# The norms of a two-layer diffusion block: high halves straight from PSUM, one weight wait more, and a regrouped product

## The chip, the cores and the metric

The kernel runs on one core of one Trainium2 chip. The metric is the device time of one execution, in microseconds (us). Before the change it is 1271.71 us, the median of three runs (1271.14 to 1274.31).

## The reference

Two layers of a hybrid block act on 256 latent tokens and 256 context tokens, each of width 1024. In each layer, an input modulated by `sc1` and `sh1` goes through one input projection to attention heads and gated DeltaNet heads, and through one output projection back; the sum is normalised. Then a squared-ReLU MLP follows, with a modulation and a norm of its own:

```python
x_lat = layer_norm(DEEPNORM_ALPHA * x_lat + g1 * y_lat, ln1_g[l], ln1_b[l])
x_lat = layer_norm(DEEPNORM_ALPHA * x_lat
                   + g2 * squared_relu_mlp(x_lat * (1.0 + sc2) + sh2, w_mlp1[l], w_mlp2[l]),
                   ln2_g[l], ln2_b[l])
```

The context goes through the same in layer 0 with modulations of its own. Layer 1 gives only the latent tokens. All is float32.

## The kernel before

**Products.** A float32 product is made of three matmuls in a rounded float32 type (fp32r): each operand is split into a high half (the value rounded) and a low half (the rest), and `mm3` (L274 on) issues high x high, one mixed term, and the other (L276, L277, L278). So every weight tile of 128x1024 goes through `wload` (L244 on): a DMA into `wraw` (4 buffers), a copy on ScalarE that rounds it to `whi` (L250), and a subtraction on VectorE that gives `wlo` (L252). There are 3 buffers of whi and wlo, and 6 more that can be filled ahead of a stage (NHOLD). 224 weights go this way.

**Tiles.** The 512 tokens are four tiles `t` of 128; t = 0 and 1 are context, t = 2 and 3 latent. Token-major products write PSUM tiles `pst` (128x512, two halves of the width per tile), and `z_update` (L1054 on) adds them to the residual x on VectorE in two instructions (`ztmp` at L1058, x at L1060 or L1062), here called z rows.

**The norm.** `ln` (L390 on) takes the statistics of x on VectorE (L394, L396, L399), `rs` on GpSimd (POOL), `nm` on VectorE (L411). Then the first half of x is normalised on ScalarE (L414) and the second on VectorE (L415). TensorE transposes x in eight 128x128 pieces into two PSUM tiles `lnp`, one for each half, each a bank (L422). Out of these comes the next product's operand, modulated per column by A and B: a float32 copy `lnh`, of which the first half is written by ScalarE in four pieces (L427) and the second by VectorE in four pieces (L429). From lnh, ScalarE makes the high half `hhi`, 128x512 at a time (L433), and VectorE the low half `hlo` (L434). Ten norms do this: layer 0's first norm for four tiles, its second norm for four, layer 1's first norm for t = 2 and 3. Afterwards `affine` (L439, L440) applies the norm's own gain and bias to x with VectorE, off the way to the product.

**The order.** A list scheduler puts the instructions of each engine into one static queue. An edge, `tc.issue_after`, can hold an instruction behind another in the queue without any data between them: `fence` (L251, L412, L1057) holds the instructions of VectorE that are traced after a norm behind that norm's nm. A bit mask in CFG says which: 1 is wlo, 2 is ztmp. `f12` is the mask of layer 1's first norm, t = 2; `f13` that of t = 3, `f02` that of layer 0's, t = 3 (keys (1, 1, 2) and so on in L412).

**The product after layer 1's first norm.** For t = 2 and 3 the first four weights of the MLP are used token-major (`mlp1_tok`, L1244 on): h is the stationary operand of 24 matmuls of 128x512 into one PSUM tile `pm1`, with two pieces k of h per weight and `mm3` for each k. The remaining weights follow in 128x256 products.

**MLP rows.** In the MLP, ScalarE and VectorE turn `pm` into `ah` and `al` (mr at L1239 and al at L1242 on VectorE).

Of the kernel before, what the change touches and what calls it, by code (L numbers as in the profile page):

```python
# [15 lines left out]
AF = mybir.ActivationFunctionType  # L16
ALU = mybir.AluOpType
# [5 lines left out]
KT = 8  # L23
# [17 lines left out]
    "ord0": "HHBHHCXfNffffNNfffffNKQffaaaKaQfaaKfaQfaffaaKfaQfaZaaaZZfffafffZ",  # L41
    "ord1": "BHHHHCNfffXNfffNfNfKfQfaafKfQfaaKfQKfaQfaafffZZZaZ", "tr": 7, "tr2": 2, "acc": 2, "g": 3, "n": 3,
    "late": 3, "tord": (0, 1, 2, 3), "adab": "n", "depth": 3, "npre": 8, "pre1": (0, 2, 3), "vt": "n",
    "tm": 1, "tmh": (2, 3), "gt": 2, "f02": 1, "f12": 2, "f13": 1,
    "start": "WLmmmWme01WLmmmm2eLmbm0mmbLe1m2m0mme12012bb", "cin": 7, "rows": 1,
}
C_ID, C_U, C_L, C_CM, C_COS, C_SIN, C_END = 0, 128, 256, 384, 448, 704, 960
# [129 lines left out]
def body(ctx, tc, a, out, dump=None):  # L177
    nc = tc.nc
    V, S, G, PE, SP = nc.vector, nc.scalar, nc.gpsimd, nc.tensor, nc.sync
# [47 lines left out]
    def small(shape, name, dt=F32, bufs=3):  # L227
        return P0.tile(shape, dt, name=name, tag="sm_" + name, bufs=bufs)
# [44 lines left out]
    last_mm = []  # L273

    def mm3(o, l, r, start, stop):
        PE.matmul(o, l[0], r[0], start=start, stop=False)  # L276
        PE.matmul(o, l[0], r[1], start=False, stop=False)  # L277
        last_mm[:] = [PE.matmul(o, l[1], r[0], start=False, stop=stop).ins]  # L278

    def new_h(pool, n=NTOK):  # L280
        return (pool.tile([128, KT, n], F32R, name="hhi", tag="hhi"),
                pool.tile([128, KT, n], F32R, name="hlo", tag="hlo"))
# [104 lines left out]
    def seg(t):  # L387
        return 1 if t < 2 else 0

    def ln(MP, l, which, t, z, cols, h, c_=0, fin=None):  # L390
# [6 lines left out]
        rs = small([128, 1], "rs")  # L397
# [15 lines left out]
        n = z  # L413
        S.activation(n[:, :512], z[:, :512], AF.Identity, bias=nm, scale=rs)  # L414
        V.tensor_scalar(n[:, 512:], z[:, 512:], rs, nm, op0=ALU.mult, op1=ALU.add)  # L415
        if h is not None:
            A, B = cols
            s = seg(t)
            for i in range(2):
                p = sn("lnp").rearrange("p (j c) -> p j c", j=4)  # L420
                for j in range(4):
                    PE.transpose(p[:, j], n[:, 512 * i + 128 * j:512 * i + 128 * j + 128], ident)  # L422
                hf = MP.tile([128, 4, 128], F32, name="lnh", tag="lnh", bufs=2)
                for j in range(4):
                    k = 4 * i + j
                    if i == 0:
                        S.activation(hf[:, j], p[:, j], AF.Identity, bias=B[:, s, k:k + 1], scale=A[:, s, k:k + 1])  # L427
                    else:
                        V.tensor_scalar(hf[:, j], p[:, j], A[:, s, k:k + 1], B[:, s, k:k + 1], op0=ALU.mult, op1=ALU.add)  # L429
                c0 = 128 * t - c_  # L430
                dh = h[0][:, 4 * i:4 * i + 4, c0:c0 + 128]
                dl = h[1][:, 4 * i:4 * i + 4, c0:c0 + 128]
                S.activation(dh, hf, AF.Copy)  # L433
                V.tensor_tensor(dl, hf, dh.bitcast(F32), op=ALU.subtract)  # L434

    def affine(x, rows):
# [671 lines left out]
    with tc.tile_pool(name="xin", bufs=1, reuse_waits="tile") as XP, \  # L1108
# [30 lines left out]
        with tc.manual_schedule(engines={nc.tensor.engine}):  # L1139
            for c in CFG["start"]:  # L1140
                i = cnt.get(c, 0)
# [29 lines left out]
    for l in range(L):  # L1171
# [9 lines left out]
        with tc.tile_pool(name="mlp%d" % l, bufs=1, reuse_waits="tile") as MP:  # L1181
# [27 lines left out]
            A, B, sh = mod_cols(l, 2)  # L1209
            fuse_cols(A, B, sh, l, 0)  # L1210
            h2 = new_h(MP, width)
# [32 lines left out]
            def mlp1_tok(ws, t):  # L1244
                c0 = 128 * t - t0
                ps = sm("pm1")
                for i in range(4):
                    for k2 in range(2):
                        k, c = 2 * i + k2, slice(512 * k2, 512 * k2 + 512)
                        mm3(ps, (h2[0][:, k, c0:c0 + 128], h2[1][:, k, c0:c0 + 128]), (ws[i][0][:, c], ws[i][1][:, c]), k == 0, k == KT - 1)  # L1250
                r = MP.tile([128, 512], F32, name="mrt", tag="ztmp", bufs=2)
                S.activation(r, ps, AF.Relu)
                V.tensor_tensor(r, r, r, op=ALU.mult)
                return t, r, last_mm[0]
# [108 lines left out]
```

## Time and profile before

| | |
|---|---|
| median of 3 runs | 1271.71 us (1271.14 to 1274.31) |
| the profiled execution | 1274.56 us, its span 1272.8 us |
| TensorE / VectorE / ScalarE / GpSimd busy | 96% / 68% / 49% / 7% |
| mean granted clock of TensorE | 0.981 |
| chain of work that ended last | TensorE 75%, VectorE 10%, ScalarE 5% |
| largest group on VectorE | wlo, L252, 224 times, 275.5 us |
| largest group on ScalarE | whi, L250, 224 times, 237.0 us |

The profile is of one execution. Its span is what lies between its first and its last instruction, and the execution takes 1.8 us more than that. TensorE's clock has two levels, 2.4 GHz and 1.2 GHz, and the column PEclk gives what was granted as a share of the full one. In a timeline, a row's start and duration stand first; "x4" merges four instructions that follow each other, and the bracket at the end names an idle time before the row and what ended it. Rows of one engine can overlap a little, as an instruction's end lies after the start of the next.

### The profile page before, as it was taken

Reading aid. Unit: us, or ns where it says so; the run is one execution under the profiler, and the core shown is the slowest. Engines: PE = TensorE matmul, PEld = TensorE weight load, DVE = VectorE, ACT = ScalarE, POOL = GpSimd, SP = SyncE. Lnnn points to the kernel's source line nnn. Section 1 sums busy time; section 2 is a strip of 40 time slices with the busy share of each in tenths; the row PEclk is TensorE's granted clock in tenths of the full one; section 3 lists DMA queues with packets and bytes.
Section 4 is the critical chain, followed back from the end, with each engine's and each line's share of the span. In section 5 each row is a group of like instructions: output and inputs, shape, how many; then the busy total and the mean of one; then the engine's idle time right before and its main releaser. Section 6 shows DMA issues by size and latency. Waiting matters only on the chain.

```text
span 1272.8 us, 20344 instructions
## 1 busy us (share of the span) xinstructions
PE 1217.7 (96%) x7848; PEld 988.5 (78%) x7848; DVE 862.5 (68%) x1716; ACT 619.0 (49%) x1131; POOL 90.2 (7%) x98
## 2 busy tenths in 40 slices
PE   7999899999999999999999999899899998999997
PEld 3676568887878987787788889675578886898996
DVE  4798497766479954444444588994876768766677
ACT  2465737665446632322322456567455654544552
POOL 0133000100101000000000001221000110000000
PEclk9999998999999999999999999999889998999999
DMA  9624470215166633534533355236621357455562
GB/s 329 225 67 129 148 251 19 63 50 183 63 230 190 222 120 118 160 127 130 158 128 100 100 182 199 70 113 203 219 89 36 112 177 280 166 185 195 183 187 95
DMA packets 62721, 190.92 MB, mean 150 GB/s; under 512 B 7808, under 2 KB 17824, under 8 KB 62624
## 3 DMA queue, kind: packets, MB, share of 16 engines
q1 hardware_dynamic: 62624, 189.62, 45.4%
q8 instruction: 62, 1.02, 0.3%
q14 instruction: 35, 0.29, 0.1%
HBM read 187.46 MB, written 2.13 MB: 149 GB/s over the span
## 4 chain that ended last, share of the span: by engine, by line
PE 75%; DVE 10%; ACT 5%; POOL 2%; issue 2%; DMA 2%; SPq 0%; DVEq 0%; POOLq 0%; ACTq 0%
PE pst L276 8%; PE pst L277 8%; PE pst L278 8%; PE pm L276 7%; PE pm L278 7%; PE pm L277 7%; PE pss L717 3%; PE adaps L303 3%; DVE wlo L252 2%; PE pss L697 1%; DVE XT L533 1%; PE psn L276 1%; PE pss L714 1%; PE psn L278 1%; ACT MY L822 1%
## 5 line engine op out<-in xcount | busy, mean ns | idle before, releaser
L252 DVE TENSOR_TENSOR wlo<-wraw,whi 128x1024 fp32r<-128x1024 f32 x224 | 275.5, 1232 | 187.6 <-ACT whi L250 187.0
L250 ACT ACTIVATE whi<-wraw 128x1024 fp32r<-128x1024 f32 x224 | 237.0, 1060 | 316.8 <-PE pst L278 172.0
L276 PE MATMUL pm<-hhi,whi 128*128 128x256 f32 (+1 forms) x544 | 176.4, 324 | 0.8 <-ACT whi L250 0.7
L278 PE MATMUL pm<-hhi,wlo 128*128 128x256 f32 (+1 forms) x544 | 174.5, 321 | 0.0
L277 PE MATMUL pm<-hlo,whi 128*128 128x256 f32 (+1 forms) x544 | 174.4, 321 | 0.0
L276 PE MATMUL pst<-whi,ah 128*128 128x512 f32 x384 | 150.0, 391 | 0.0
L277 PE MATMUL pst<-wlo,ah 128*128 128x512 f32 x384 | 149.5, 389 | 0.0
L278 PE MATMUL pst<-whi,al 128*128 128x512 f32 x384 | 149.1, 389 | 0.0
L276 PEld LDWEIGHTS pm<-hhi,whi 128*128 128x128 f32 x544 | 103.5, 190 | 14.4 <-issue 5.8
L278 PEld LDWEIGHTS pm<-hhi,wlo 128*128 128x128 f32 x544 | 103.6, 190 | 7.8
L277 PEld LDWEIGHTS pm<-hlo,whi 128*128 128x128 f32 x544 | 103.6, 190 | 7.2
L276 PEld LDWEIGHTS pst<-whi,ah 128*128 128x128 f32 x384 | 72.1, 188 | 15.5 <-issue 0.8
L278 PEld LDWEIGHTS pst<-whi,al 128*128 128x128 f32 x384 | 72.1, 188 | 15.1
L277 PEld LDWEIGHTS pst<-wlo,ah 128*128 128x128 f32 x384 | 72.1, 188 | 14.5
L276 PE MATMUL psg<-hhi,whi 128*128 128x512 f32 (+1 forms) x216 | 78.1, 363 | 4.7 <-ACT XT L531 2.3
L277 PE MATMUL psg<-hlo,whi 128*128 128x512 f32 (+1 forms) x216 | 78.1, 362 | 0.2 <-DVE hlo L1119 0.2
L278 PE MATMUL psg<-hhi,wlo 128*128 128x512 f32 (+1 forms) x216 | 77.9, 361 | 0.4 <-DVE wlo L252 0.4
L533 DVE SCALAR_TENSOR_TENSOR XT<-U,cw,XT 128x512 f32<-128x512 f32 (+1 forms) x96 | 67.4, 723 | 1.9 <-ACT XT L531 1.6
L1241 ACT ACTIVATE ah<-mr 128x256 fp32r<-128x256 f32 (+1 forms) x68 | 33.4, 492 | 65.6 <-DVE mr L1239 65.6
L303 PE MATMUL adaps<-wraw,scT 128*32 128x256 f32 x640 | 56.4, 395 | 3.4 <-DMA wraw<-w_ada 3.2
L231 POOL TENSOR_TENSOR rs<-ve,mh 128x1 f32<-128x1 f32 x12 | 12.5, 1043 | 630.9 <-DVE bmv L396 362.2
L1242 DVE TENSOR_TENSOR al<-mr,ah 128x256 fp32r<-128x256 f32 (+1 forms) x68 | 35.1, 517 | 24.3 <-ACT ah L1241 24.2
(671 smaller groups left out, 2418.8 us busy)
## 6 DMA issues: line engine op xcount, KB each, us to landing
wraw<-w SPq DMA_DIRECT2D x140, 512.0 KB
wraw<-w_ada SPq DMA_DIRECT2D x80, 512.0 KB
wraw<-w_gdn SPq DMA_DIRECT2D x27, 512.0 KB
wraw<-w_out SPq DMA_DIRECT2D x24, 512.0 KB
xa<-w_ada SPq DMA_DIRECT2D x32, 256.0 KB
wraw<-w_vz SPq DMA_DIRECT2D x16, 512.0 KB
wraw<-w_na SPq DMA_DIRECT2D x16, 512.0 KB
lnrow<-lnr SPq DMA_DIRECT2D x8, 512.0 KB
```

Of the source, the lines that this page charges most:

```text
L250: S.activation(hi, r, AF.Copy)
L252: V.tensor_tensor(lo, r, hi.bitcast(F32), op=ALU.subtract)
L276: PE.matmul(o, l[0], r[0], start=start, stop=False)
L277: PE.matmul(o, l[0], r[1], start=False, stop=False)
L278: last_mm[:] = [PE.matmul(o, l[1], r[0], start=False, stop=stop).ins]
L303: PE.matmul(st["ps"][32 * g:32 * g + 32, :256], scT[:, k, :], w[:, 256 * g:256 * g + 256], start=(k == 0), stop=(k == 7), tile_position=(0 ...
L533: V.scalar_tensor_tensor(av, cin[:, sg:, kk:kk + 256], cw[:, b, kk:kk + 1], av, op0=ALU.mult, op1=ALU.add)
L697: PE.matmul(ps[:, :128 * nkt], nqT[hp][:, a2, qs], nkT[hp][i][:, a2, :128 * nkt], start=i == 0, stop=i == 1)
L714: PE.transpose(ps[:, 128 * kt_:128 * kt_ + 128], p_[:, 128 * kt_:128 * kt_ + 128], ident)
L717: PE.matmul(ps[:, 0:65], p_[:, 128 * kt_:128 * kt_ + 128], nv[:, kt_, hd], start=kt_ == 0, stop=kt_ == nkt - 1)
L1241: S.activation(ah, r, AF.Copy)
L1242: V.tensor_tensor(al, r, ah.bitcast(F32), op=ALU.subtract)
```

## The change

Three things are changed. In `ln`, both halves are now treated alike: for each of the eight pieces ScalarE writes hhi straight out of PSUM (L438 of the changed kernel), VectorE writes lnh out of the same PSUM piece (L439), and hlo is subtracted as before (L440). CFG sets f12 to 3, so that the three wlo that are traced after t = 2's norm in layer 1 come behind its nm as well as the ztmp. And `mlp1_tok` issues, for two weights at a time (four column pieces), first the products with hhi and then the four with hlo.

```diff
-    "tm": 1, "tmh": (2, 3), "gt": 2, "f02": 1, "f12": 2, "f13": 1,
+    "tm": 1, "tmh": (2, 3), "gt": 2, "f02": 1, "f12": 3, "f13": 1,
...
+    def mm3_of(o, ls, rs, start, stop):
+
+        n = len(ls)
+        for i in range(n):
+            PE.matmul(o, ls[i][0], rs[i][0], start=start and i == 0, stop=False)
+            PE.matmul(o, ls[i][0], rs[i][1], start=False, stop=False)
+        for i in range(n):
+            last_mm[:] = [PE.matmul(o, ls[i][1], rs[i][0], start=False, stop=stop and i == n - 1).ins]
...
                 hf = MP.tile([128, 4, 128], F32, name="lnh", tag="lnh", bufs=2)
-                for j in range(4):
-                    k = 4 * i + j
-                    if i == 0:
-                        S.activation(hf[:, j], p[:, j], AF.Identity, bias=B[:, s, k:k + 1], scale=A[:, s, k:k + 1])
-                    else:
-                        V.tensor_scalar(hf[:, j], p[:, j], A[:, s, k:k + 1], B[:, s, k:k + 1], op0=ALU.mult, op1=ALU.add)
                 c0 = 128 * t - c_
                 dh = h[0][:, 4 * i:4 * i + 4, c0:c0 + 128]
                 dl = h[1][:, 4 * i:4 * i + 4, c0:c0 + 128]
-                S.activation(dh, hf, AF.Copy)
+                for j in range(4):
+                    k = 4 * i + j
+                    S.activation(dh[:, j], p[:, j], AF.Identity, bias=B[:, s, k:k + 1], scale=A[:, s, k:k + 1])
+                    V.tensor_scalar(hf[:, j], p[:, j], A[:, s, k:k + 1], B[:, s, k:k + 1], op0=ALU.mult, op1=ALU.add)
                 V.tensor_tensor(dl, hf, dh.bitcast(F32), op=ALU.subtract)
...
-                for i in range(4):
-                    for k2 in range(2):
-                        k, c = 2 * i + k2, slice(512 * k2, 512 * k2 + 512)
-                        mm3(ps, (h2[0][:, k, c0:c0 + 128], h2[1][:, k, c0:c0 + 128]), (ws[i][0][:, c], ws[i][1][:, c]), k == 0, k == KT - 1)
+                for i in range(0, 4, 2):
+                    ls = [(h2[0][:, k, c0:c0 + 128], h2[1][:, k, c0:c0 + 128]) for k in range(2 * i, 2 * i + 4)]
+                    rs = [(ws[j][0][:, c:c + 512], ws[j][1][:, c:c + 512]) for j in (i, i + 1) for c in (0, 512)]
+                    mm3_of(ps, ls, rs, i == 0, i == 2)
```

Three places in the queues show what it does to the order. The number at the end of a name tells instances apart, and the words in brackets name the engines or DMA queues whose semaphores the instruction waits for.

VectorE in layer 0's second norm, t = 0 and 1, up to the weight that TensorE needs next (wlo_6886 in the kernel before). Before:

```order
L434 TENSOR_TENSOR hlo_6566<-lnh_6745,hhi_6565 128x4x128 [waits Activation_49]
L252 TENSOR_TENSOR wlo_6860<-wraw_6857,whi_6859 128x1024 [waits DMAHW3_49,Activation_49]
L434 TENSOR_TENSOR hlo_6566<-lnh_6757,hhi_6565 128x4x128 [waits Activation_49]
L1058 TENSOR_TENSOR ztmp_6875<-pst2_6801,grow_4711 128x512 [waits PE_49]
L429 TENSOR_SCALAR lnh_6794<-lnp_6789,mA_6559,mB_6560 128x128 [waits DVE_49]
L429 TENSOR_SCALAR lnh_6794<-lnp_6789,mA_6559,mB_6560 128x128 x2
L434 TENSOR_TENSOR hlo_6566<-lnh_6782,hhi_6565 128x4x128 [waits Activation_49]
L429 TENSOR_SCALAR lnh_6794<-lnp_6789,mA_6559,mB_6560 128x128
L1062 TENSOR_TENSOR x2_3615<-x2_3615,ztmp_6875 128x512 [waits DVE_49]
L1058 TENSOR_TENSOR ztmp_6878<-pst2_6802,grow_4711 128x512 [waits PE_49]
L252 TENSOR_TENSOR wlo_6886<-wraw_6883,whi_6885 128x1024 [waits DMAHW4_49]
```

After, where the same weight is wlo_6922:

```order
L1064 TENSOR_TENSOR ztmp_6911<-pst2_6837,grow_4735 128x512
L439 TENSOR_SCALAR lnh_6812<-lnp_6807,mA_6583,mB_6584 128x128 [waits Activation_49]
L439 TENSOR_SCALAR lnh_6827<-lnp_6822,mA_6583,mB_6584 128x128 [waits Activation_49]
L1068 TENSOR_TENSOR x2_3615<-x2_3615,ztmp_6911 128x512 [waits DVE_49]
L439 TENSOR_SCALAR lnh_6812<-lnp_6807,mA_6583,mB_6584 128x128 [waits Activation_49]
L439 TENSOR_SCALAR lnh_6827<-lnp_6822,mA_6583,mB_6584 128x128 [waits Activation_49]
L440 TENSOR_TENSOR hlo_6590<-lnh_6812,hhi_6589 128x4x128 [waits DVE_49]
L439 TENSOR_SCALAR lnh_6827<-lnp_6822,mA_6583,mB_6584 128x128 [waits Activation_49]
L1064 TENSOR_TENSOR ztmp_6914<-pst2_6838,grow_4735 128x512
L440 TENSOR_TENSOR hlo_6590<-lnh_6827,hhi_6589 128x4x128 [waits DVE_49]
L1068 TENSOR_TENSOR x3_3617<-x3_3617,ztmp_6914 128x512 [waits DVE_49]
L252 TENSOR_TENSOR wlo_6922<-wraw_6919,whi_6921 128x1024 [waits DMAHW4_49]
```

Both halves of the norm stand in VectorE's queue now, piece by piece and each behind a wait for ScalarE; the weight comes behind the last hlo and the last x row, where before it stood ahead of them.

ScalarE in layer 1's first norm, t = 2. Before:

```order
L414 ACTIVATE x2_10085<-x2_10085,nm_10177,rs_10173 128x512 [waits DVE_49]
L427 ACTIVATE lnh_10186<-lnp_10181,mB_10038,mA_10037 128x128 [waits PE_49]
L427 ACTIVATE lnh_10186<-lnp_10181,mB_10038,mA_10037 128x128 x3
L433 ACTIVATE hhi_10043<-lnh_10186 128x4x128 [waits Activation_49]
L433 ACTIVATE hhi_10043<-lnh_10198 128x4x128 [waits DVE_49]
```

After:

```order
L423 ACTIVATE x2_10133<-x2_10133,nm_10225,rs_10221 128x512 [waits DVE_49]
L438 ACTIVATE hhi_10091<-lnp_10229,mB_10086,mA_10085 128x128 [waits PE_49]
L438 ACTIVATE hhi_10091<-lnp_10244,mB_10086,mA_10085 128x128 [waits PE_49]
L438 ACTIVATE hhi_10091<-lnp_10229,mB_10086,mA_10085 128x128 [waits DVE_49]
L438 ACTIVATE hhi_10091<-lnp_10244,mB_10086,mA_10085 128x128 [waits DVE_49]
L250 ACTIVATE whi_10370<-wraw_10368 128x1024 [waits DMAHW1_49]
L438 ACTIVATE hhi_10091<-lnp_10229,mB_10086,mA_10085 128x128 [waits DVE_49]
L438 ACTIVATE hhi_10091<-lnp_10244,mB_10086,mA_10085 128x128 [waits DVE_49]
```

The pieces of the two PSUM tiles (lnp_10229 and lnp_10244) take turns, and from the second piece of each on, they wait for VectorE's lnh of the piece before; a whi stands among them.

VectorE in the same norm. Before:

```order
L252 TENSOR_TENSOR wlo_10214<-wraw_10211,whi_10213 128x1024 [waits DMAHW6_49,Activation_49]
L1060 SCALAR_TENSOR_TENSOR x2_10085<-x2_10085,ztmp_10165 128x512 [waits DVE_49]
L252 TENSOR_TENSOR wlo_10220<-wraw_10217,whi_10219 128x1024 [waits DMAHW7_49,Activation_49]
L394 BN_STATS bst2_10168<-x2_10085 128x6 [waits DVE_49]
L396 BN_AGGR bmv_10171<-bst2_10168 128x2 [waits DVE_49]
L399 TENSOR_SCALAR ve_10174<-bmv_10171 128x1 [waits DVE_49]
L411 SCALAR_TENSOR_TENSOR nm_10177<-bmv_10171,rs_10173 128x1 [waits Pool_49]
L1058 TENSOR_TENSOR ztmp_10241<-pst2_10047,grow_10089 128x512
L415 TENSOR_SCALAR x2_10085<-x2_10085,rs_10173,nm_10177 128x512 [waits DVE_49]
```

After:

```order
L403 BN_STATS bst2_10216<-x2_10133 128x6 [waits DVE_49]
L405 BN_AGGR bmv_10219<-bst2_10216 128x2 [waits DVE_49]
L408 TENSOR_SCALAR ve_10222<-bmv_10219 128x1 [waits DVE_49]
L420 SCALAR_TENSOR_TENSOR nm_10225<-bmv_10219,rs_10221 128x1 [waits Pool_49]
L252 TENSOR_TENSOR wlo_10262<-wraw_10259,whi_10261 128x1024 [waits DMAHW5_49,Activation_49]
L424 TENSOR_SCALAR x2_10133<-x2_10133,rs_10221,nm_10225 128x512 [waits DVE_49]
L252 TENSOR_TENSOR wlo_10268<-wraw_10265,whi_10267 128x1024 [waits DMAHW6_49,Activation_49]
L439 TENSOR_SCALAR lnh_10234<-lnp_10229,mA_10085,mB_10086 128x128 [waits Activation_49]
L439 TENSOR_SCALAR lnh_10249<-lnp_10244,mA_10085,mB_10086 128x128 [waits Activation_49]
L252 TENSOR_TENSOR wlo_10274<-wraw_10271,whi_10273 128x1024 [waits DMAHW7_49]
```

Three wlo have moved from the rows ahead of nm to those behind it, the last of them between the norm's pieces.

## Rows read from the trace of the kernel before

**Rows 1.** The page: busy time, share of the span and instructions of each engine.

```profile
PE 1217.7 (96%) x7848; PEld 988.5 (78%) x7848; DVE 862.5 (68%) x1716; ACT 619.0 (49%) x1131; POOL 90.2 (7%) x98
```

**Rows 2.** Windows: stretch, length, busy us of five engines, PEclk, DMA share, GB/s.

```profile
370.00:450.00 80.00, 79.31 (x539) 73.12 (x538) 77.00 (x134) 49.20 (x83) 5.46 (x4) 1.00 0.63 213
...
500.00:600.00 100.00, 100.00 (x484) 77.57 (x483) 42.73 (x54) 28.10 (x35) 0.00 (x0) 1.00 0.46 141
...
1076.00:1085.00 9.00, 7.60 (x21) 5.90 (x22) 7.90 (x19) 2.83 (x7) 0.94 (x1) 0.50 0.52 203
```

**Rows 3.** TensorE's waits: engine, line, releaser; us in total, times, longest.

```profile
PE lnp L422 <- ACT x L414: 3.9, 1, 3.9
...
PE pm L276 <- ACT hhi L433: 2.1, 2, 1.4
```

**Rows 4.** Single lines of the norm: durations in ns, minimum, median and maximum.

```profile
L427 ACT ACTIVATE lnh<-lnp,mB,mA x40: 435/458/496, 387.8 to 1088.2; 128x128 f32<-128x128 f32 x40
...
L429 DVE TENSOR_SCALAR lnh<-lnp,mA,mB x40: 398/402/411, 388.5 to 1090.0; 128x128 f32<-128x128 f32 x40
...
L433 ACT ACTIVATE hhi<-lnh x20: 612/632/682, 389.9 to 1090.4; 128x512 fp32r<-128x512 f32 x20
```

**Rows 5.** Timeline (start us, us, instruction), layer 0, first norm, tiles 0 and 1.

```profile
388.45 1.37 DVE L429 TENSOR_SCALAR lnh<-lnp,mA,mB 128x128 f32<-128x128 f32 x4
...
397.28 1.21 DVE L252 TENSOR_TENSOR wlo<-wraw,whi 128x1024 fp32r<-128x1024 f32 x1
...
398.92 0.39 PE L277 MATMUL pst<-wlo,hhi 128*128 128x512 f32 x1
```

**Rows 6.** Timeline, the same norm, tiles 2 and 3.

```profile
412.22 1.36 DVE L429 TENSOR_SCALAR lnh<-lnp,mA,mB 128x128 f32<-128x128 f32 x4
...
420.79 0.42 DVE L1239 TENSOR_TENSOR mr<-mr 128x256 f32<-128x256 f32 x1
...
421.13 1.22 DVE L252 TENSOR_TENSOR wlo<-wraw,whi 128x1024 fp32r<-128x1024 f32 x1
...
423.25 0.28 PE L278 MATMUL pm<-hhi,wlo 128*128 128x256 f32 x1
```

**Rows 7.** Timeline, layer 0, second norm, tiles 0 and 1.

```profile
757.23 1.36 DVE L429 TENSOR_SCALAR lnh<-lnp,mA,mB 128x128 f32<-128x128 f32 x4
...
758.53 0.69 DVE L434 TENSOR_TENSOR hlo<-lnh,hhi 128x512 fp32r<-128x512 f32 x1
...
765.10 1.21 DVE L252 TENSOR_TENSOR wlo<-wraw,whi 128x1024 fp32r<-128x1024 f32 x1
...
766.23 0.68 DVE L434 TENSOR_TENSOR hlo<-lnh,hhi 128x512 fp32r<-128x512 f32 x1
...
766.83 0.69 DVE L1062 TENSOR_TENSOR x<-x,ztmp 128x512 f32<-128x512 f32 x1
...
766.82 0.39 PE L277 MATMUL pst<-wlo,ah 128*128 128x512 f32 x1
```

**Rows 8.** Timeline of TensorE, the same norm, tiles 2 and 3.

```profile
785.39 0.63 PE L276 MATMUL psg<-hhi,whi 128*128 128x256 f32 x3 [0.45 <-ACT hhi L433]
```

**Rows 9.** Timeline, layer 1, first norm, VectorE and then TensorE.

```profile
1074.86 0.16 DVE L411 SCALAR_TENSOR_TENSOR nm<-bmv,rs 128x1 f32<-128x1 f32 x1 [0.68 <-POOL rs L231]
...
1077.93 1.36 DVE L429 TENSOR_SCALAR lnh<-lnp,mA,mB 128x128 f32<-128x128 f32 x4 [0.65 <-PE lnp L422]
...
1084.74 0.16 DVE L411 SCALAR_TENSOR_TENSOR nm<-bmv,rs 128x1 f32<-128x1 f32 x1 [0.45 <-POOL rs L231]
...
1079.29 0.80 PE L276 MATMUL pm<-whi,hhi 128*128 128x512 f32 x1 [1.40 <-ACT hhi L433]
...
1084.58 0.62 PE L276 MATMUL pm<-whi,hhi 128*128 128x512 f32 x1
...
1094.99 0.39 PE L278 MATMUL pm<-whi,hlo 128*128 128x512 f32 x1
...
1095.22 0.60 PE L1261 MATMUL pm<-cst,mrt 128*128 128x128 f32 x4
```

## The prediction, made before the changed kernel ran

> **What bounds the kernel now.** I read the page's busy shares first: TensorE is busy 96% of the span, VectorE 68%, ScalarE 49% [rows 1]. So a gain can come only out of the 4% in which TensorE stands still, and a loss comes in wherever TensorE is made to stand. The table of windows shows that VectorE's mean hides two kinds of stretch: from 500 to 600 us it is busy 43% with TensorE at 100 of 100 us, but from 370 to 450 us, around layer 0's first norm, it is busy 77.0 of 80 us [rows 2]. There TensorE is fed just in time by the low halves of the weights (wlo), which VectorE computes. The list of TensorE's waits names the norm twice with a price: 3.9 us for the normalised x on ScalarE and 2.1 us for hhi, of which one took 1.4 us [rows 3]. This one ends at 1079.29, in layer 1's first norm [rows 9], and the clock is low there: a granted clock of 0.50 from 1076 to 1085 [rows 2], that is the 1.2 GHz level. Thirteen matmuls, the first at 1079.29 and the last at 1084.58, lie 0.44 us apart, against 0.23 at the full clock (1094.99 to 1095.22) [rows 9]. So the dip costs some 13 x 0.21 = 2.7 us beside the waits.
>
> **What the change takes and adds.** In each of the ten norms with an h, VectorE now reads all eight 128x128 pieces out of PSUM instead of four. One takes 402 ns [rows 4], but they follow each other every 0.325 us (the four from 757.23 are over by the next row at 758.53) [rows 7]. That is 1.3 us more VectorE work per norm, 13 us in all. ScalarE goes from four pieces of 458 ns and two copies of 632 ns to eight pieces [rows 4]: about the same work, on an engine half idle; and no copy stands between the piece and the first matmul, which is worth up to 0.6 us where TensorE waits for hhi. The token-major block keeps its 24 matmuls in another order; by itself that costs nothing, it only asks for hlo six matmuls later. POOL's order is the same, and SP's has two loads of lnrow one place earlier. I take nothing for these: what TensorE waits for in the norms is ScalarE's results [rows 3], and in the full stretch the DMA share is 0.46 [rows 2].
>
> The part that the diff doesn't show is a wait. In the order of the changed kernel ScalarE's piece j+1 of a half waits for VectorE's piece j of that half, and VectorE's piece j for ScalarE's piece j, because both now read one PSUM bank. Before, each bank had one reader, so no row shows the price. Its bounds: nothing, if the two banks of a norm alternate so well that no engine stands; or a full turn per piece, 0.458 + 0.402 = 0.86 us for a pair of banks in place of 2 x 0.325 = 0.65, which is 4 x 0.21 = 0.84 us per norm [rows 4, 7]. A wlo (1.13 us) or a whi that stands between two pieces in either queue holds the other engine as well and could cost more. I take the 0.84, the nearest to what the rows time.
>
> The Trainium skill speaks for a price: its page "PSUM — Partial Sum Buffer", in the section on bank collisions that raise a hardware error, says that two engines may not touch one bank in the same partitions at one time, reads against reads included, so that software has to order them. The trace of before can only agree, as no bank has two readers there. By this rule the sum is the 19.5 us below; if turns cost nothing, it is the 11.1.
>
> **Stage by stage.** I laid the new VectorE queue out by hand with these spacings: lnh 0.325; wlo 1.13 (765.10 to 766.23); hlo 0.60 (to 766.83), and a z row (ztmp or x, of the same size) the same [rows 7]; an MLP row (mr or al) 0.34 (420.79 to 421.13) [rows 6]. First the work alone.
>
> *Layer 0, first norm, t = 0 and 1.* The wlo that TensorE first uses at 398.92 began at 397.28 [rows 5]. Now it stands behind all 16 lnh (5.20), one wlo (1.13), three hlo (1.80) and four z rows (2.40): 10.5 us after 388.45 it begins, at 399.0, and ends 1.21 later at 400.2. TensorE is 1.3 us late, and VectorE 1.7 behind.
>
> *The same norm, t = 2 and 3.* The wlo used at 423.25 began at 421.13 [rows 6]. Now the pieces begin at 412.22 + 1.13 (a wlo put ahead) - 0.34 (an al put behind) = 413.0; ahead of the wlo are 15 lnh (4.88), seven MLP rows (2.38), one wlo and three hlo, 10.2 us. It ends at 424.4, and at 426.1 with the 1.7 that VectorE brings along, as it has 3 idle us in 80 [rows 2]: 2.8 late, the first 1.3 included.
>
> *Layer 0, second norm, t = 0 and 1.* From 757.23 on, 16 lnh, one wlo, four hlo and four z rows are 11.1 us, so the wlo used at 766.82 begins at 768.4 in place of 765.10 and ends at 769.6: 2.8 late [rows 7].
>
> *The same, t = 2 and 3.* Eight more lnh are 2.6 us. TensorE already waits 0.45 us for hhi there, at 785.39 [rows 8], so no work of its own hides them: 2.6 late, if VectorE has no idle time to put them in, which I assume.
>
> *Layer 1, first norm.* Here lies the gain: the two wlo that stood ahead of t = 2's statistics go behind its nm, which comes some 2.0 us earlier than at 1074.86. But all three wlo (3.4), four lnh (1.3) and one affine row (0.6) now lie between it and nm of t = 3. The two nm are 9.88 us apart in before [rows 9], of which VectorE stood still 0.65 for the transposes (at 1077.93) and 0.45 for POOL, so 8.8 + 5.3 = 14.1 now, with these filled: nm of t = 3 comes at 1086.9, 2.2 later than at 1084.74. Behind it come four more lnh (1.3) less the copy (0.6), and the block of t = 3, over at 1095.22 in before, is 2.9 late. What is gained at the start is lost to the second tile.
>
> **Sum.** By work alone 2.8 + 2.8 + 2.6 + 2.9 = 11.1 us; the turns of ten norms add 10 x 0.84 = 8.4: 19.5 us. Nothing gives it back: between the stages TensorE is full (100 of 100 us, rows 2), so a late start stays late. The profiled execution took 1274.56 us, 2.85 above the median of 1271.71; against itself the sum gives 1294.1, on the median 1291.2. I say **1291**.
>
> **The rivals.**
> - *Turns are free.* The alternation hides itself and only VectorE's extra work counts: 1271.7 + 11.1 = 1282.8. For it: two banks are always in play. Against it: rows of wlo and whi stand between the pieces.
> - *Faster: layer 1 decides.* If the weights that TensorE holds cover VectorE's lag in layer 0, and t = 3's norm hides behind t = 2's block, then the start comes 2.0 earlier, the copy (0.6) goes, and so do the 2.7 us at half clock, as the wait is shorter: 1271.7 - 5.3 = 1266.4. It decides from the point where a wlo is ready 3 us before its first use; in the three that I followed it is over 0.4, 0.9 and 0.5 us before [rows 5 to 7]. The wait of 3.9 us is real, so I don't dismiss it.
> - *Both signs cancel.* Layer 0 loses some 3 us and layer 1 gains about as many: 1268 to 1275.
> - *The clock falls in each stage.* If each of the four new stalls brings a dip like that at 1076, four times 2.7 come on top: 1291.2 + 10.8 = 1302.0.
> - *The change doesn't do what it says.* This has one place: nm of t = 2 moves up, but the x that waits for it stands behind a whi in ScalarE's queue, so that less than the 2.0 us may reach TensorE. That takes up to 2 us from the gain and is within the forecast's range.
>
> **How the numbers follow.** The forecast (1284 to 1299) gets 0.58; turns free 0.14; the clock falling everywhere 0.08; faster 0.14; cancelled 0.06. About 0.3% is what a measurement of this kernel can tell from no change, so "same" is 1268 to 1275.5. Faster 0.14, same 0.06, slower 0.58 + 0.14 + 0.08 = 0.80. To hold eight in ten, the range goes from 1267, which leaves out half of the faster cases, to 1303, just past the clock's rival. The slower cases alone span 1280 to 1303.
>
> **What would show it.** The changed profile should list 80 lnh on VectorE in place of 40, and waits of ScalarE for lnh and of VectorE for hhi that before doesn't have. TensorE should wait for wlo or hlo in the stretches around 400, 425, 768 and 785 us, some 3 to 5 us in each of the two norms of layer 0 per pair of tiles. In layer 1 the wait for x should shrink from 3.9 us to about 2, and the second tile's block should end some 4 us later than 1095.22, counted from the same start of the norm. If TensorE shows no wait for a wlo in layer 0, the first terms of the sum are wrong; if VectorE and ScalarE never wait for each other's pieces, the 8.4 is wrong; if the clock holds at 1.00 from 1076 to 1085, the loss in layer 1 is too high by up to 2.7.

## The result, and the profile after

The changed kernel takes 1292.14 us (median of four runs, 1290.78 to 1293.68) against 1271.45 of the kernel before (four runs): a ratio of 1.0158, with a 95% interval of 1.0143 to 1.0174. It is 20.7 us slower; 1291 was forecast. The profiled execution took 1291.09 us.

The page's busy shares after, to be held against [rows 1]:

```profile
PE 1221.3 (95%) x7848; PEld 988.5 (77%) x7848; DVE 873.4 (68%) x1756; ACT 625.2 (49%) x1151; POOL 91.3 (7%) x98
```

VectorE has 40 instructions and 10.9 us more (13 us were forecast), ScalarE 20 and 6.2 us more; TensorE does the same matmuls in a longer span. The averages say little else.

TensorE's waits around the norms after (engine, line and tile, what it waited for: us in total, times, longest), against [rows 3]:

```profile
PE lnp L431 <- ACT x L423: 5.6, 3, 2.8
...
PE lnp L431 <- DVE lnh L439: 2.4, 2, 1.2
...
PE pm L284 <- ACT hhi L438: 2.3, 2, 1.9
...
PE pm L276 <- ACT mr L1244: 1.9, 2, 1.1
...
PE psg L276 <- ACT whi L250: 1.8, 2, 1.0
...
PE psg L277 <- DVE hlo L440: 1.4, 1, 1.4
PE pm L277 <- DVE hlo L440: 1.4, 1, 1.4
PE pm L287 <- DVE hlo L440: 1.3, 2, 0.8
...
PE pst L277 <- DVE wlo L252: 1.1, 1, 1.1
```

Before, the norms had the waits for x and for hhi and little more. Now TensorE waits for all that passes through the two queues: for hlo, for wlo and whi, for the MLP's mr, and, with the transposes (lnp L431), for VectorE to give the PSUM tile free (2.4 us). The wait for x has become three.

The turns on the shared bank have rows of their own, VectorE's wait and ScalarE's:

```profile
DVE lnh L439 <- ACT hhi L438: 2.8, 10, 0.6
```

```profile
ACT hhi L438 <- DVE lnh L439: 6.1, 13, 0.7
```

How they look in layer 1's norm, t = 2: ScalarE's timeline (start us, us, instruction, idle time before it and what ended it), then VectorE's, in the changed kernel:

```profile
1086.85 0.90 ACT L438 ACTIVATE hhi<-lnp,mB,mA 128x128 fp32r<-128x128 f32 x2 [0.75 <-PE lnp L431]
1087.96 0.81 ACT L438 ACTIVATE hhi<-lnp,mB,mA 128x128 fp32r<-128x128 f32 x2 [0.21 <-DVE lnh L439]
1089.68 1.06 ACT L250 ACTIVATE whi<-wraw 128x1024 fp32r<-128x1024 f32 x1 [0.91 <-DMA wraw<-w]
1090.65 1.73 ACT L438 ACTIVATE hhi<-lnp,mB,mA 128x128 fp32r<-128x128 f32 x4
...
1089.30 0.72 DVE L439 TENSOR_SCALAR lnh<-lnp,mA,mB 128x128 f32<-128x128 f32 x2
1089.94 0.68 DVE L1064 TENSOR_TENSOR ztmp<-pst,grow 128x512 f32<-128x512 f32 x1
1091.12 0.76 DVE L439 TENSOR_SCALAR lnh<-lnp,mA,mB 128x128 f32<-128x128 f32 x2 [0.51 <-ACT hhi L438]
```

A whi whose transfer landed late stands between the pieces on ScalarE, and holds not only the next hhi but VectorE's next lnh as well.

**Where the time went.** Both programs have 7848 matmuls, some of them in another order within a stretch, so the k-th matmul of one trace can be held against the k-th of the other where both have the same one. These eight rows of the changed kernel's TensorE timeline are the matmuls that in before start at 380.11, 410.03, 450.01, 755.21, 775.03, 796.09, 1060.09 and 1102.11 us:

```profile
376.48 0.39 PE L277 MATMUL pst<-wlo,hhi 128*128 128x512 f32 x1
...
411.11 0.28 PE L277 MATMUL pm<-hlo,whi 128*128 128x256 f32 x1
...
453.94 0.28 PE L276 MATMUL pm<-hhi,whi 128*128 128x256 f32 x1
...
759.17 0.39 PE L278 MATMUL pst<-whi,al 128*128 128x512 f32 x1
...
783.87 0.28 PE L277 MATMUL psg<-hlo,whi 128*128 128x256 f32 x1
...
809.91 0.28 PE L460 MATMUL psba<-hlo,wbr 128*32 128x256 f32 x1
...
1071.96 0.39 PE L278 MATMUL pst<-whi,hlo 128*128 128x512 f32 x1
...
1118.36 0.28 PE L278 MATMUL pm<-hhi,wlo 128*128 128x256 f32 x1
```

The changed kernel is 3.6 us ahead at the first, 1.1 behind at the second, 3.9 at the third and 4.0 at the fourth, and so on. The difference from one to the next is what a stretch lost. The table has these for all runs (us, each number rounded by itself; A and B are layer 0's first norm, t = 0, 1 and t = 2, 3; C and D its second norm; E layer 1's first norm; from 450 to 755 and behind 1102 nothing moves). "D to E" is the work between the norms, which the change doesn't touch: there the traces differ by -3.9 to +3.5 us, with dips of the clock at other places (before is at 0.84 from 905 to 960, the changed kernel at 0.87 over the same matmuls), so no cause is read from that column. Ahead of the first of the eight matmuls the traces differ too, by -3.6 to +1.5 us, in runs that change nothing there (e11 is 3.5 ahead), so the 3.6 us are not read as a gain of the change either.

```
run                    A     B     C     D   D to E    E    norms A+B+C+D+E
changed kernel       +4.7  +2.9  +4.9  +5.0   -2.0   +4.4    21.8
e1 norm only         +4.5  +2.8  +4.0  +5.8   -2.6   +3.4    20.5
e2 f12 only           0.0   0.0   0.0   0.0   +2.3   +2.6     2.5
e3 block only         0.0   0.0   0.0   0.0   -3.9   +0.1     0.1
e4 no turns          +4.6  +6.5  +4.9  +0.4   -3.5   +2.4    18.8
e5 work alone        +1.4  +3.9  +4.3  +1.0   -1.9   +1.6    12.1
e6 turns alone       +0.2  +2.6  +1.1  +1.6   +3.5   +5.2    10.7
e7 blocks            +3.9  +5.7  +3.2  +0.3   -2.8   +1.6    14.6
e8 scalar twice      -0.5  +2.6  +0.8  -0.4   -1.9   -0.2     2.4
e9 late affine       +0.1   0.0   0.0   0.0   -1.2   -0.2    -0.2
e10 e9 with f12       0.0   0.0   0.0   0.0   -2.3   +1.0     0.9
e11 e10, ScalarE      0.0   0.0   0.0   0.0   -0.6   +0.3     0.3
e12 change, blocks   +3.8  +5.7  +3.2  +0.3   +0.7   +4.9    17.9
```

All five stretches of the norms lose, 21.8 us in all, about the timed difference of 20.7. The two traces as wholes differ by less, 16.3 us, because of the 3.6 ahead of A and the 2.0 between D and E.

TensorE's idle times in three of them, changed kernel, against [rows 5], [rows 7] and [rows 8]:

```profile
396.94 0.38 PE L277 MATMUL pm<-hlo,whi 128*128 128x256 f32 x1 [1.36 <-DVE hlo L440]
398.41 0.61 PE L277 MATMUL pst<-wlo,hhi 128*128 128x512 f32 x1 [1.08 <-DVE wlo L252]
...
765.73 0.66 PE L431 MATMUL lnp<-cst,x 128*128 128x128 f32 x4 [1.18 <-DVE lnh L439]
...
794.34 0.92 PE L431 MATMUL lnp<-cst,x 128*128 128x128 f32 x4 [1.20 <-DVE lnh L439]
799.94 0.39 PE L277 MATMUL psg<-hlo,whi 128*128 128x256 f32 x1 [1.39 <-DVE hlo L440]
```

And the clock, in the windows behind these idle times (stretch, its us, busy us of the engines, PEclk, DMA share, GB/s):

```profile
396.00:400.00 4.00, 1.97 (x5) 1.48 (x6) 4.00 (x6) 0.46 (x1) 0.00 (x0) 0.83 0.17 39
400.00:404.00 4.00, 4.00 (x15) 3.16 (x15) 2.69 (x5) 1.06 (x1) 0.00 (x0) 0.74 0.84 294
...
420.00:430.00 10.00, 8.94 (x72) 8.56 (x71) 9.69 (x21) 6.57 (x15) 0.00 (x0) 1.00 0.64 203
...
765.00:770.00 5.00, 3.67 (x12) 2.78 (x13) 5.00 (x13) 3.39 (x8) 0.00 (x0) 0.73 0.32 105
...
795.00:800.00 5.00, 3.61 (x20) 2.69 (x18) 4.44 (x12) 2.88 (x7) 0.00 (x0) 0.70 0.58 221
...
1094.00:1098.00 4.00, 3.98 (x9) 2.58 (x9) 4.00 (x9) 0.00 (x0) 0.00 (x0) 0.50 0.81 315
```

In A, C and D a dip has come that before doesn't have; B stays at 1.00. Full clock missing is 4 x 0.17 + 4 x 0.26 = 1.7 us in A, and about as much in C and D (5 x 0.27 and 5 x 0.30, and a little beside). It is time lost: TensorE works all through these dips, and in A the nine matmuls from 398.41 to 401.81 start 0.43 us apart, where they started 0.23 apart before. So some 5.1 us of the 17.4 that layer 0 loses are the clock's. The other traces have such dips in other stretches: e1 in A and D, e4 in A, B and C, e5 in C, e7 and e12 in A and B, and e2, e3, e6 and e8 to e11 in none of layer 0's. Each is 1.7 us of the table.

Layer 1, TensorE and VectorE's two nm, changed kernel, against [rows 9]:

```profile
1086.16 1.09 PE L431 MATMUL lnp<-cst,x 128*128 128x128 f32 x8 [2.25 <-ACT x L423]
...
1091.14 0.50 PE L284 MATMUL pm<-whi,hhi 128*128 128x512 f32 x1 [1.93 <-ACT hhi L438]
...
1100.82 1.70 PE L431 MATMUL lnp<-cst,x 128*128 128x128 f32 x8 [2.84 <-ACT x L423]
...
1084.71 0.16 DVE L420 SCALAR_TENSOR_TENSOR nm<-bmv,rs 128x1 f32<-128x1 f32 x1 [0.68 <-POOL rs L231]
...
1099.76 0.16 DVE L420 SCALAR_TENSOR_TENSOR nm<-bmv,rs 128x1 f32<-128x1 f32 x1 [0.45 <-POOL rs L231]
```

TensorE enters this stretch 11.9 us later than in before. With that taken off, nm of t = 2 comes at 1072.8, 2.0 us earlier than before, and nm of t = 3 at 1087.9, 3.1 later. The wait for x of t = 2 has gone from 3.9 to 2.25 us, and t = 3 has a new one of 2.84. The block of t = 3 ends 4.7 us later than before, counted the same way (1111.82 - 11.87 against the 1095.22 of [rows 9]).

### The profile page after: what moved, and what is told of

Its sections match the earlier page's. It is cut to its first block, busy times and chain, and to the rows that moved or that the text cites. A ratio compares the mean times of both kernels' runs of the same rounds, so it can differ in the third digit from the quotient of the medians.

```text
span 1289.0 us, 20405 instructions
## 1 busy us (share of the span) xinstructions
PE 1221.3 (95%) x7848; PEld 988.5 (77%) x7848; DVE 873.4 (68%) x1756; ACT 625.2 (49%) x1151; POOL 91.3 (7%) x98
## 4 chain that ended last, share of the span: by engine, by line
PE 74%; DVE 11%; ACT 5%; POOL 2%; issue 2%; DMA 2%; SPq 0%; DVEq 0%; ACTq 0%; POOLq 0%
PE pst L277 8%; PE pst L278 8%; PE pst L276 8%; PE pm L276 7%; PE pm L278 7%; PE pm L277 7%; PE pss L723 3%; PE adaps L312 3%; DVE wlo L252 2%; ACT whi L250 1%; PE pss L703 1%; PE psn L276 1%; DVE XT L539 1%; PE pss L720 1%; PE psn L278 1%
## 5 line engine op out<-in xcount | busy, mean ns | idle before, releaser
L276 PEld LDWEIGHTS pm<-hhi,whi 128*128 128x128 f32 x544 | 103.5, 190 | 16.5 <-issue 5.8
L276 PEld LDWEIGHTS psg<-hhi,whi 128*128 128x128 f32 x216 | 41.7, 193 | 14.2 <-ACT XT L537 3.3
```

## The experiments

The theory was: VectorE's added work delays what TensorE waits for, the turns on one PSUM bank add to it, and what f12 gains in layer 1 is lost to the second tile. The rivals were that the weights' wait is the loss, that turns are free, and that the work is hidden. Times are medians; each ratio is to the kernel before, run beside it, whose own medians are 1271.8 to 1273.0 us there; differences in us are to these. The expectations were worked out from 1271.5. One reservation holds for all of them: each edit makes the list scheduler lay out the queues anew, so rows that the edit doesn't name move as well. No run keeps the order of before with the work of the change, so the price of the order by itself is not separated from that of the work and the turns.

**e1, the norm alone** (f12 and the token-major block as before):

```diff
-    "tm": 1, "tmh": (2, 3), "gt": 2, "f02": 1, "f12": 3, "f13": 1,
+    "tm": 1, "tmh": (2, 3), "gt": 2, "f02": 1, "f12": 2, "f13": 1,
```

> The norm's change alone (f12 stays 2, the token-major block as before). Theory: the loss is VectorE's four more pieces per norm and the turns on one PSUM bank, so nearly all of the 20.7 us stays: 1271.5 + 17 to 20 = 1288 to 1292, with some 17 us of it in layer 0. Rival, the weight wait in layer 1 is what costs: 1280 or less.

Measured: 1292.4 us, ratio 1.0164 (1.0129 to 1.0200), just above the range; 17.1 us of the table's 20.5 lie in layer 0. The norm's edit alone makes a loss as large as the whole change. In layer 1 the block in its old order stands 4.4 and 2.2 us for hlo; in the changed kernel, in the new order, 0.5 and 0.8. So the regrouping may well matter once hlo is late; no run has it with the norm's edit and f12 = 2.

**e2, f12 = 3 alone; e3, the token-major block alone.**

> Only f12 = 3: the three wlo behind nm of t = 2, the norm as before. Theory: t = 2 starts some 2 us earlier and t = 3's nm comes some 1.5 to 3 us later, since 3.4 us of wlo now lie between the two; 1270 to 1274. Rival, the wait is the loss: 1276 or more. Rival, it is a gain that the norms eat up: 1268 or less.

> Only the token-major block in its new order (hhi products first), everything else as before. Theory: hlo is asked for six matmuls later, but TensorE waits for hhi there, not hlo; 1270.5 to 1272, no difference that can be measured.

Measured: e2 1275.3 us, ratio 1.0019 (0.9999 to 1.0039); e3 1273.6 us, ratio 1.0004 (0.9984 to 1.0024). Both lie above their ranges, but neither can be told from no change by its time. The trace tells e2 apart: TensorE's idle times in layer 1's norm,

```profile
1076.43 0.66 PE L431 MATMUL lnp<-cst,x 128*128 128x128 f32 x4 [1.86 <-ACT x L423]
...
1090.84 1.54 PE L431 MATMUL lnp<-cst,x 128*128 128x128 f32 x6 [4.02 <-ACT x L423]
```

The first wait is 2.0 us shorter than the 3.9 of [rows 3], and a wait of 4.0 us for the second tile's x has come in its place: 2.6 us lost in all. A part of this is the clock: TensorE stands 7.5 us in E against 6.1 in before, and the granted clock of the stretch is 0.85 against 0.88. The prediction's account of the order of things in layer 1 stands, without any turns in it.

**e4, no turns.** VectorE writes all eight lnh, ScalarE copies each finished half (the norm's edit against the changed kernel; f12 and the block as before):

```diff
-                    S.activation(dh[:, j], p[:, j], AF.Identity, bias=B[:, s, k:k + 1], scale=A[:, s, k:k + 1])
                     V.tensor_scalar(hf[:, j], p[:, j], A[:, s, k:k + 1], B[:, s, k:k + 1], op0=ALU.mult, op1=ALU.add)
+                S.activation(dh, hf, AF.Copy)
```

> VectorE writes all eight float32 pieces from PSUM, as in the change, but ScalarE makes hhi by a copy of the finished half in SBUF (as before), so no PSUM bank has two readers; f12 and the block as before. It has the extra work on VectorE without the turns. Theory: work alone, 1271.5 + 8 to 12 = 1280 to 1284, some 8 us below the norm's change alone. Rival, turns are free and the work is all: as the norm's change alone (1288 to 1292). Rival, the extra work fits into VectorE's idle time and the turns are all: 1273 or less.

Measured: 1288.1 us, ratio 1.0123 (1.0093 to 1.0153), above what the theory allowed and at the foot of the range of the rival that turns are free. But this kernel has more in it than the work: hhi of the first half now waits for four VectorE pieces and a copy. It loses most where a wlo is late, 11.1 us in A and B (3.4 of it the clock's), and 0.4 in D. So it neither separates the two terms nor refutes that rival; e5 and e6 do that better.

**e5, the work alone.** The norm as before, but VectorE reads the second half's pieces once more into a tile that nobody uses:

```diff
+                if i == 1:
+                    again = MP.tile([128, 128], F32, name="again", tag="again", bufs=1)
+                    for j in range(4):
+                        k = 4 * i + j
+                        V.tensor_scalar(again, p[:, j], A[:, s, k:k + 1], B[:, s, k:k + 1], op0=ALU.mult, op1=ALU.add)
```

> The norm as before, but VectorE reads the second half's four pieces once more into a tile that nobody uses: the 13 us of VectorE work that the change adds, with no bank read by two engines and nothing that waits for the extra pieces. Theory (work 11.1 of the 19.5): 1272 + 8 to 12 = 1280 to 1284, lost in the same stages of layer 0. Rival, VectorE's idle time takes it and the change's loss is all turns: 1275 or less. Rival, the work is the whole loss: 1289 or more.

Measured: 1285.8 us, ratio 1.0091 (1.0057 to 1.0126), or 13.5 us, between the theory's range and the rival's; 12.1 in the stretches, of which 1.7 is a dip of the clock in C. Nothing uses these values, and still TensorE stands. Three of its rows:

```profile
400.71 0.50 PE L277 MATMUL pst<-wlo,hhi 128*128 128x512 f32 x1 [0.88 <-DVE wlo L252]
425.06 0.39 PE L276 MATMUL pm<-hhi,whi 128*128 128x256 f32 x1 [2.26 <-ACT mr L1252]
...
794.31 0.30 PE L468 MATMUL psba<-hhi,wbr 128*32 128x256 f32 x1 [1.45 <-DVE again L446]
```

VectorE's queue is full, and what stands in it behind the pieces comes late. The third row shows that the run isn't quite what was meant: no one needs the values, but in D a matmul waits 1.45 us for a read into `again`, and this is most of D's loss. The rival that the work is hidden falls; so does the one that work is all, since 8.4 us of e1's 20.5 are left over.

**e6, the turns alone.** First half as before; in the second ScalarE writes hhi from the bank that VectorE reads, with no more work on VectorE:

```diff
                     if i == 0:
                         S.activation(hf[:, j], p[:, j], AF.Identity, bias=B[:, s, k:k + 1], scale=A[:, s, k:k + 1])
                     else:
+                        S.activation(dh[:, j], p[:, j], AF.Identity, bias=B[:, s, k:k + 1], scale=A[:, s, k:k + 1])
                         V.tensor_scalar(hf[:, j], p[:, j], A[:, s, k:k + 1], B[:, s, k:k + 1], op0=ALU.mult, op1=ALU.add)
...
-                S.activation(dh, hf, AF.Copy)
+                if i == 0:
+                    S.activation(dh, hf, AF.Copy)
```

> No more work on VectorE: the first half is as before (ScalarE writes lnh, then copies hhi), in the second half ScalarE writes hhi from PSUM piece by piece while VectorE writes lnh from the same bank. Only the turns (one bank in each norm instead of two) are new. Theory (0.84 us a norm for two banks): 4 to 9 us, 1276 to 1281. Rival, turns are free: 1274 or less.

Measured: 1288.8 us, ratio 1.0118 (1.0082 to 1.0155): 16.5 us, far more than expected, and by its time not to be told from e1 or e5. Its trace accounts for 10.7, in an execution of 1285.2 us, the lowest of its four; what the others lost beside is not seen. VectorE's waits and ScalarE's in it:

```profile
DVE lnh L442 <- ACT hhi L441: 5.8, 11, 1.2
```

```profile
ACT hhi L441 <- DVE lnh L442: 4.8, 8, 1.0
```

With one shared bank there is no second bank to go on with, and each single wait is longer (VectorE 5.8 us in 11, ScalarE 4.8 in 8, against 2.8 in 10 and 6.1 in 13 in the changed kernel). Turns are not free. Half of the loss, 5.2 us, is in layer 1, where the token-major block in its old order asks for hlo at its third matmul and waits 2.8 us for it. TensorE stands 8.5 us there, 2.4 more than in before; most of the rest is the clock, 0.82 over the stretch against 0.88.

**e7, blocks**: four hhi first, then four lnh, in e1's kernel; **e12** is the same in the whole change.

```diff
                 for j in range(4):
                     k = 4 * i + j
                     S.activation(dh[:, j], p[:, j], AF.Identity, bias=B[:, s, k:k + 1], scale=A[:, s, k:k + 1])
+                for j in range(4):
+                    k = 4 * i + j
                     V.tensor_scalar(hf[:, j], p[:, j], A[:, s, k:k + 1], B[:, s, k:k + 1], op0=ALU.mult, op1=ALU.add)
```

> The norm's change, f12 and the token-major block as before, but in each half ScalarE writes its four hhi pieces first and VectorE its four lnh pieces after, so that the bank changes hands once instead of seven times. Same work. Theory: most of the turns' price goes and the work stays, 1282 to 1287, 5 to 10 us below the norm's change alone (1292.4). Rival, the work is the whole loss: 1290 to 1294.

> The whole change (f12 = 3 and the new token-major block too) with each half read in blocks: four hhi on ScalarE, then four lnh on VectorE, so one hand-over of the bank per half. If the turns' price is in the number of hand-overs, the norms' stretches add up to some 13 to 16 us in the trace in place of the change's 21.8, and the whole takes 1283 to 1288. If it is in the order of VectorE's queue and in ScalarE being first at each bank, however often it changes hands: 19 to 22 us in the stretches and 1290 to 1294.

Measured: e7 1291.0 us, ratio 1.0143 (1.0105 to 1.0181); e12 1290.3, ratio 1.0134 (1.0108 to 1.0160). By time neither differs from e1 or from the change, and both lie where the rivals had them. By the traces layer 0 loses 13.0 us in both, against 17.1 and 17.4. D costs 0.3 in place of 5.8 and 5.0, and B 5.7 in place of 2.8 and 2.9; 1.7 us of each of these shifts is a dip of the clock that D no longer has and B now has. In layer 1 e12 has a wait of its own of 6.9 us for the second tile's x:

```profile
1099.30 1.97 PE L431 MATMUL lnp<-cst,x 128*128 128x128 f32 x8 [6.86 <-ACT x L423]
```

The stretches of e12 add up to 17.9 us, between its two ranges. So the number of hand-overs may be a part of the price, but not all of it, and what is saved in one stretch is spent in another. How much exactly can't be settled with these runs.

**e8, ScalarE twice.** In the first half ScalarE writes hhi and then lnh from PSUM; VectorE and the second half as before, with the block's new order:

```diff
+                if i == 0:
+                    for j in range(4):
+                        k = 4 * i + j
+                        S.activation(dh[:, j], p[:, j], AF.Identity, bias=B[:, s, k:k + 1], scale=A[:, s, k:k + 1])
+                    for j in range(4):
+                        k = 4 * i + j
+                        S.activation(hf[:, j], p[:, j], AF.Identity, bias=B[:, s, k:k + 1], scale=A[:, s, k:k + 1])
...
```

> ScalarE writes the first half's hhi straight from PSUM and then its lnh from PSUM as well, VectorE and the second half are as before, so VectorE has no more work and no bank has two readers; the token-major block has its new order, f12 = 2. ScalarE gets 0.9 us more per norm. Theory: the direct high half costs nothing once VectorE is left alone; hhi of the first half comes up to 0.6 us earlier where TensorE waits for it: 1269 to 1273. Rival, reading PSUM directly is itself slow or ScalarE has become the bound: 1277 or more.

Measured: 1275.9 us, ratio 1.0024 (1.0007 to 1.0041), between the two expectations. With VectorE's work left as it was and no bank shared, 18 of the 20.5 us are gone; 2.6 us are left in B. There the wlo stand at other places in VectorE's queue than in before, though the edit doesn't touch them. The direct write itself thus costs little: 2.4 us in the stretches at most, with the new order in them.

**e9 to e11, a way to keep f12's gain.** The affine rows of layer 1 go behind nm of t = 3 (e9); with f12 = 3 and the block's new order (e10); with e8's norm in layer 1 as well (e11).

```diff
-                    affine(xr[t], rows[0])
+                    with tc.issue_after(fence[-1][0]) if last else nullcontext():
+                        affine(xr[t], rows[0])
```

> The kernel before with one edit: in layer 1 the affine rows of x (eight of 0.6 us on VectorE) are queued behind nm of t = 3. Theory, VectorE's work between the two nm sets when t = 3 can start: nm of t = 3 comes 1.2 to 1.8 us earlier, and TensorE's wait of 0.7 us ahead of t = 3's block goes: layer 1's norm 0.5 to 1.5 us shorter in the trace, the whole 1270.5 to 1272.5. Rival, something else sets it: no change in the stage.

> As the last one, with f12 = 3 and the token-major block in its new order; the norm as before. Theory: f12 = 3 lost 2.6 us in layer 1's norm because 3.4 us of wlo fell between the two nm; with the affine rows out of that stretch at least 1.2 of it comes back: the stage within -1 and +1.5 of before, the whole 1270 to 1274. Rival, the wlo are late for the block of t = 2 itself: +2.5 in the stage as for f12 = 3 alone.

> As the last one, and in layer 1 alone ScalarE writes the first half's hhi and lnh both from PSUM (no bank with two readers, no more VectorE work). Theory: the copy of 0.6 us goes from ahead of each block: the stage 0.6 to 1.5 us shorter than in the last one, 1269.5 to 1273. Rival, ScalarE's four more pieces delay the second half's hhi, and the stage doesn't get shorter.

Measured: 1275.1, 1273.1 and 1274.6 us, ratios 1.0014 (0.9990 to 1.0038), 1.0006 (0.9986 to 1.0026) and 1.0021 (1.0001 to 1.0041): none beats the kernel before, and only e10 is within its range. In the traces e9 moves nm of t = 3 from 1084.74 to

```profile
1083.42 0.16 DVE L411 SCALAR_TENSOR_TENSOR nm<-bmv,rs 128x1 f32<-128x1 f32 x1 [0.67 <-POOL rs L231]
```

and gains 0.2 us: TensorE's queue has the second tile's transposes among the first tile's matmuls, at 1085.71, where x isn't waited for, and the wait of 0.7 us behind them stays, so the theory was wrong there. A new wait comes instead, for an mr of the MLP:

```profile
1099.40 0.39 PE L276 MATMUL pm<-hhi,whi 128*128 128x256 f32 x1 [1.03 <-ACT mr L1239]
```

With f12 = 3, where that x is late, e10 takes the stretch's loss from e2's 2.6 to 1.0 us, the amount expected. The wait for x falls from 4.0 to 2.95, but e9's new wait is there too, and TensorE stands as long as in e2 (7.6 us against 7.5); what comes back is the clock, 0.92 over the stretch against 0.85. So the loss fell for another reason than the one given, and the block's new order, which e2 hasn't, isn't separated from it. ScalarE's direct write (e11) takes the loss to 0.3. The gain of f12 is worth nothing net in any of these.

## Why the prediction was right, and where not

- **The sum.** 19.5 us were forecast, 20.7 timed, 21.8 read in the five stretches. By stretch (work and two norms' turns): A 1.3 + 1.7 = 3.0, measured 4.7; B 1.5 + 1.7 = 3.2, measured 2.9; C 4.5, measured 4.9; D 4.3, measured 5.0; E 4.6, measured 4.4. In A, C and D 1.7 us each are the clock's dip, which the sum had at nothing and left to a rival. Without the dips layer 0 lost 3.0, 2.9, 3.2 and 3.3, or 12.3 us, where 15.0 were forecast. So the total fits because work and turns were sized too high in C and D and the clock was left out; that is luck.
- **What TensorE waited for.** The sum had a wlo late in A, B and C. In the changed kernel A has that wait (1.08, with 1.36 for hlo); B waits for mr instead (1.06 and 0.82), and C for transposes and a product held up by lnh (1.18 and 0.60) and for a whi (0.97). The prediction laid all of it on VectorE's queue; a part of what came late, mr and whi, stood in ScalarE's, whose pieces now wait for VectorE's.
- **The work term** (11.1) held as a whole: e5 measured 12.1 in the stretches, 10.4 without its dip of the clock, though with f12 = 2, so without the three wlo between the two nm; these alone are e2's 2.6. Its split was less good: B measured 3.9 and D 1.0, where 1.5 and 2.6 were forecast. In D VectorE had idle time after all (before has it busy 17.8 of 21 us from 775 to 796), and what was lost there is the wait for `again`.
- **The turns' term** (8.4) has the size of e1 less e5, 20.5 - 12.1 = 8.4, and this agreement to 0.1 us is luck too. 1.7 us of it is the clock, as e1 has one dip more in layer 0 than e5; and e1 differs from e5 in more than the turns, since in it hlo of the first half needs VectorE's pieces. The mechanism was mis-told as well. 0.84 us per norm was priced as VectorE standing; in the trace VectorE stands only 2.8 us for hhi in all ten norms, and ScalarE 6.1 for lnh. The loss comes as late hhi, late whi and mr behind them on ScalarE, and as transposes that wait for a tile which two engines must leave. One shared bank (e6) costs 10.7 us in the stretches, about half of what the change costs.
- **A row for the price.** The prediction says that before has no bank with two readers. That holds for the norms only. Elsewhere the kernel before reads a PSUM tile (`psn`) with both engines, ScalarE at L745 and VectorE at L746, and ScalarE waits there (us in total, times, longest):

```profile
ACT QS L745 <- DVE QS L746: 6.4, 4, 2.9
```

Whether the bank or the data ends these waits, the row doesn't tell, but it shows waits several times as long as a piece, and could have widened the bounds set for the turns.

- **The rule of the Trainium skill** ("PSUM — Partial Sum Buffer", section "PSUM bank collisions raise a hardware error"), by which the two engines may not touch the bank at once and software has to order them: the trace agrees in that ScalarE's and VectorE's pieces wait for each other 23 times, 2.8 + 6.1 us. These waits are semaphores that the program holds; that the hardware would do harm without them, no run here shows.
- **The clock.** The rival said a dip in every new stall, 2.7 us each. Three came, in A, C and D, at 1.7 us; B has none, and layer 1's is about as long as before, in two parts.
- **Layer 1.** nm of t = 2 came 2.0 us earlier (2.0 forecast), the wait for x fell by 1.6 (less than 2.0, as the late whi made likely), nm of t = 3 came 3.1 later (2.2 forecast without turns), the second block ended 4.7 later (some 4), the stretch lost 4.4 (4.6). Here the order of events came out as told.
- **Giving back.** "Nothing gives it back" holds between 450 and 755 us (0.0). Between D and E the changed kernel gains 2.0, inside the scatter of that column.
- The rival of a gain named slack of 3 us as its condition. The slack wasn't there: e5's pieces, whose values nobody needs, stopped TensorE.

## What to carry to other kernels

Count what an edit adds to the queue of an engine in the stretch where that engine is full, not over the span: in e5, 13 us of VectorE work at a mean of 68% busy cost 12 us, 1.7 of them by the clock, since it lay where VectorE was busy 77 of 80 us (around the first norm) and 37 of 41 (around the second) and rows that TensorE needed stood behind it. Before two engines are set to read one PSUM bank, ask what stands in each queue between the pieces, since the other engine now waits for that as well. And where a chain is moved up by pushing other work behind it, look at the next tile's chain first: it is the one that the pushed work delays.

## What the runs showed of the hardware that was not expected

The durations of the pieces in the changed kernel (ns: minimum, median, maximum), against [rows 4]:

```profile
L438 ACT ACTIVATE hhi<-lnp,mB,mA x80: 437/457/507, 384.1 to 1107.5; 128x128 fp32r<-128x128 f32 x80
...
L439 DVE TENSOR_SCALAR lnh<-lnp,mA,mB x80: 396/405/414, 384.7 to 1108.0; 128x128 f32<-128x128 f32 x80
```

Writing the rounded high half from PSUM takes ScalarE 457 ns per 128x128 piece, the same as the 458 ns of the float32 piece. VectorE's piece from the shared bank takes 405 ns against 402: the reads are not slower, the price lies in the waits and the order.

And idle times of the same length did not always bring the clock down. In C, e1 and the changed kernel stand nearly alike, 1.15 and 0.60 us against 1.18 and 0.60; from 765 to 770 the changed kernel's clock was 0.73 (above), e1's 1.00 (stretch, its us, busy us of the engines, PEclk, DMA share, GB/s):

```profile
765.00:770.00 5.00, 3.61 (x17) 2.78 (x17) 5.00 (x13) 3.40 (x8) 0.00 (x0) 1.00 0.30 105
```

In e5 the unbroken idle time of 2.26 us ahead of 425.06 left the clock at 1.00, while two shorter ones, 0.69 and 0.99 us, around 775 were followed by a dip:

```profile
420.00:430.00 10.00, 7.58 (x61) 7.17 (x60) 9.59 (x20) 6.41 (x13) 0.00 (x0) 1.00 0.35 91
776.00:780.00 4.00, 4.00 (x12) 3.08 (x12) 3.51 (x5) 0.34 (x1) 0.00 (x0) 0.57 0.70 212
```

So a stall of a microsecond or two sometimes cost its own length and sometimes 1.7 us more; what decides it, these runs don't show.
